# Decayed cumulative sum of a matmul: a new written order for the last 30 slots, and the last two output blocks copied in two pieces each

## The chip, the cores and the metric

The kernel runs on one core of a Trainium2 chip. The metric is the device time of one execution in microseconds (us). PE is the matrix engine, DVE the vector engine, ACT the scalar engine, POOL the GpSimd engine, and SP the engine whose queue issues the output stores here.

## The reference

```python
# x: (16, 2048, 1024), w: (1024, 1024), decay: (1024,), all float32
xw = x @ w
out[:, 0, :] = xw[:, 0, :]
for t in range(1, S):
    out[:, t, :] = decay[None, :] * out[:, t - 1, :] + xw[:, t, :]
```

A matrix product, and along the time axis of each batch a first-order recurrence with one decay per output column.

## The kernel before

**Tiling.** The time axis of each of the 16 batches is cut into 4 chunks of 512 rows: 64 chunks, numbered 0 to 63. Two neighbouring chunks make a group of 1024 rows, and each group is worked through in 8 **slots**, one for every 128 output columns. The last group is not worked in pairs: chunk 62 and chunk 63 get 8 slots each, of 512 rows ("half slots"). That makes 31 x 8 + 16 = 264 slots. In the agenda the last ones are numbered from the end: slots -32 to -17 are full, slots -16 to -1 are half.

**Input.** `load` (line 105, issued from POOL's queue) brings a quarter of a chunk as bf16 into `xb`. `turn` (line 115, DVE, letter T with the chunk's number) transposes it in 32 x 32 blocks into `xw`, and `part` (line 123, ACT, letters X and Y for the two halves) copies it into `xt`, the form that the matmul takes. `L` issues the next load, if one is left.

**Matmul.** `matmul` (line 131) makes 16 instructions of 128 x 512 for a full slot, 8 for a half slot, into PSUM. Full slots take turns on three `ps` buffers. Half slots take turns on the same three, except each fourth one (slots -13, -9, -5), which takes `spare`. PE may thus begin a full slot only when the slot three before it has left its buffer; slot -14 takes the buffer of slot -17.

**After the matmul**, a slot goes one of two ways.

- *Solo*: DVE scans all elements straight from PSUM (`run`, line 221, letter S).
- *Paired*: the recurrence is taken over every second element with the square of the decay. ACT copies the PSUM tile to `xs` (`copy`, line 183, letter p) and makes decay times its even-numbered elements into `h` (`odd`, line 169, letter g); then the PSUM buffer is free. POOL adds `h` to the odd elements (`join`, line 196, letter j), DVE scans half as many elements (line 201, letter S), ACT multiplies the result by the decay (`even`, line 169, letter h), and POOL adds the even elements (`fill`, line 246, letter c). `zero` (letter z) first sets the start element of the tile: with a POOL memset (line 190) at the start of a batch, otherwise with an ACT copy (line 192).

In both ways ACT saves the last column for the next chunk (`save`, line 250, letter k), where there is one. `back` (line 258, DVE, letter B) transposes the finished tile `so` back into an output tile `ot`; when the four slots of an outlet are back, four stores (line 279) go out on SP's queue. The tiles have rings: `so` 4, `xs` 3, `h` 4, `ot` 4 buffers.

Every fourth slot is solo by rule; `flips` turns a slot's way around.

```python
            self.paired = n % R != R - 1
            if len(tiles) in flips or len(tiles) - len(slots) in flips:
                self.paired = not self.paired
```

**Order.** Each engine runs its instructions in the order in which the program records them. While slot s is being multiplied, the deeds of its entry in `agenda` are recorded, as a string: "S-25 c-27" means the scan of slot -25, then the fill of slot -27. Slots without an entry follow `usual`, the steady pattern: copy, odd, zero and join of slot s, the scan of the slot before, and so on, then the turns and parts that are due (`later`).

**Ending.** The last four half slots (-4 to -1) are not transposed by DVE. `ending` (letter V) transposes them on PE into four blocks of 128 rows x 512 columns in PSUM (`cross`, line 383), and `leave` copies each block to SBUF (line 387; ACT for blocks 0 and 2, DVE for 1 and 3) and stores it (line 389). Slot -1 is multiplied and scanned in two halves (letters a and b).

Of the kernel before, what the change touches and what calls it, by code (L numbers as in the profile page):

```python
# [14 lines left out]
def _ap(ap_obj: bass.AP, new_ap, extra_offset=0):  # L15
    return dataclasses.replace(
        ap_obj,
        ap=[list(p) for p in new_ap],
        offset=ap_obj.offset + extra_offset,
    )  # L20
# [5 lines left out]
def kernel(  # L26
# [26 lines left out]
    nc = tc.nc  # L53
    pin = tc.keep_in_program_order
    B, S, D = x.shape
    assert w.shape == (D, D)

    NQ = 4
# [7 lines left out]
    R = K // 2  # L66
# [9 lines left out]
    def ring(pool, name, count, shape, dtype=FP32):  # L76
        i = turns[name] = turns.get(name, -1) + 1
        return pool.tile(shape, dtype, name=f"{name}{i % count}")
# [62 lines left out]
    class Tile:  # L141
# [39 lines left out]
        def copy(self):  # L181
            self.xs = sb.tile([128, 2 * TL], FP32, name=f"xs{self.lot % 3}")[:, 0:self.T]
            pin(nc.scalar.copy(out=self.xs, in_=self.ps))  # L183
# [141 lines left out]
    for q in range(NQ):  # L325
        pin(nc.sync.dma_start(
            out=rows[q * P:q * P + R],
            in_=_ap(decay, [[P, R], [CH, 2], [1, P]], q * CR)))
# [42 lines left out]
    def ending(i):  # L371
        b, t0 = chunks[-1]
        nb = TL // 128
        pts = [ring(psp, name, count, [128, R, 128])
               for name, count in (("spare1", 1), ("ps", 3), ("ps", 3), ("spare", 1))]
        wides = [ring(sb, *spot, [128, NQ, R, P])
                 for spot in (("xb", 3), ("xb", 3), ("xb", 3), ("h", 4))]

        def cross(blocks, rs):
            for i in blocks:  # L380
                for r in rs:
                    t = 2 + i * 128
                    pin(nc.tensor.transpose(  # L383
                        out=pts[i][:, r], in_=tiles[r - R].so[:, t:t + 128], identity=ident))

        def leave(i, copy):
            pin(copy(out=wides[i].rearrange("p q r i -> p r q i"),
                     in_=pts[i].rearrange("p r (q i) -> p r q i", q=NQ)))
            pin(nc.sync.dma_start(
                out=_ap(out, [[D, 128], [1, CH]], (b * S + t0 + i * 128) * D + CH),  # L390
                in_=wides[i].rearrange("p q r i -> p (q r i)")))

        cross((0,), range(R))
        cross((1,), range(R))
        cross((2, 3), range(R - 1))
        cross((2, 3), (R - 1,))
        for i in range(nb):
            leave(i, (nc.scalar.copy, nc.vector.tensor_copy)[i % 2])

    slots = [(g, n) for g in groups[:-1] for n in range(K)]  # L400
    slots += [([c], n) for c in groups[-1] for n in range(K)]
    tiles = []

    def turn_and_load(c):
# [4 lines left out]
    loads = [(c, q) for c in (2, 3, 4) for q in range(NQ)]  # L409
# [33 lines left out]
    agenda = {  # L443
        -99: "M0 M1 U0 M2 M3 U1 U2 w0 W1 w2 W3 K0 K1 K2 K3 E0 E1 G0 E2 G1 E3 F2 G3 E4 E5 G4 E6 G5 E7 F6 G7 W4 w5 W6 W7 D E8 E9 G8 E10 G9 E11 F10 G11 E12 L E13 G12 L E14 G13 E15 L F14 G15",
        0: "p0 z0 W8 W9 W10 W11",
        1: "g0",
        2: "L S1 L",
        3: "p2 z2 L g2 j0 S3 w12 w13 L w14 L w15 k1",
        4: "j2 B1 d k3",
        5: "p4 L S0 L g4 S2 L k0 h0 j4 B3 h2",  # L450
        6: "k2 c0 T2 c2 p5 g5 B0 L X2 L",
# [24 lines left out]
        31: "h28 p30 c28 B26 g30 h29 B28 j30 z30",  # L476
        32: "c29 S31 S30 h30 B29 c30 p32 g32 z32 j32 B30 B31 L L",
        33: "p33 g33 z33 j33 S32 h32 c32 k32 L L",
        -20: "z-20",
        -19: "p-20 g-20",  # L480
        -18: "j-20 S-19 S-20 k-19 B-19",
        -17: "h-20 k-20 c-20 S-18 B-20 k-18",
        -16: "I S-17",
        -15: "z-15 B-18 k-17",
        -14: "p-15 g-15 B-17 z-14 j-15",
        -13: "p-14 S-16 g-14 j-14 S-15 k-16",
        -12: "S-13 h-15 k-15 c-15 S-14 k-13",
        -11: "p-12 B-13 h-14 B-15 g-12 c-14 k-14 B-16",
        -10: "j-12 B-14 z-12 S-12 z-10 S-11",
        -9: "p-10 k-12 g-10 h-12 B-11 j-10 k-11",  # L490
        -8: "S-9 c-12 S-10 k-9",
        -7: "z-7 B-12 h-10 k-10 B-9 c-10 S-8",
        -6: "p-7 g-7 B-10 j-7 B-8",
        -5: "S-7 S-6 h-7 c-7",
        -4: "z-4 S-5 B-7",
        -3: "p-4 B-6 g-4 B-5 j-4",
        -2: "S-3 S-4",
        -1: "S-2 h-4 c-4 a-1 b-1 V",
    }
    flips = (1, 13, 15, -19, -18, -16, -11, -8, -6, -3, -2)  # L500
    later = {}
    begun = {"T": 12, "X": 11, "Y": 11}
    for c in range(5, nch):
# [6 lines left out]
    def usual(s):  # L510
        paired = [t.paired for t in tiles]
        do = [f"P{s}"] if paired[s] else []
        if paired[s - 1]:
            do.append(f"S{s - 1}")
        if not paired[s]:
            do.append(f"S{s}")
        do.append(f"C{s - 1}")
        if paired[s - 2]:
            do.append(f"B{s - 2}")
        if not paired[s - 1]:  # L520
            do.append(f"B{s - 1}")
        return do + later.get(s, []) + ["L"] * (2 if len(loads) > NQ else 1)

    def rest(s):
        do = [f"S{s - 1}"] if tiles[s - 1].paired else []
        do.append(f"C{s - 1}")
        if tiles[s - 2].paired:
            do.append(f"B{s - 2}")
        return do + [f"B{s - 1}"] + later.get(s, []) + ["L"] * len(loads)

    def perform(do):
        for deed in do:
# [4 lines left out]
    for step, (g, n) in enumerate(slots):  # L537
        T = TL * len(g)
        left = step - len(slots)
        if n % R == 0:  # L540
            ns, nj = range(n, n + R), T // P
            outlets = [Outlet(ns, nj)]
        if left == -R:
            outlets = []
        if step == 0:
            heads = [ring(psp, "ps", 3, [128, T]) for _ in range(3)]
            firsts = [ps[:, 0:TL] for ps in heads] + [spares[0]]
            seconds = [ps[:, TL:T] for ps in heads] + [spares[1]]
            for j0, j1 in halves:
                for k in range(0, K, 2):  # L550
                    for i in range(R):
                        matmul(firsts[i], i, k, xt_of[0], j0 * P, j1 * P, pairs=xw_of[0])
            for k in range(1, K, 2):
                for i in range(R):
                    matmul(firsts[i], i, k, xt_of[0])
            for k0 in range(0, K, 2):
                for i in range(R):
                    for k in (k0, k0 + 1):
                        matmul(seconds[i], i, k, xt_of[1], 0, H * P,
                               pairs=xw_of[1] if k0 < 4 else None)  # L560
            for i in range(R):
                for k in range(K):
                    matmul(seconds[i], i, k, xt_of[1], H * P, TL, H * P,
                           pairs=xw_of[1] if i < 2 else None)
        if step < R:
            ps = heads[n] if n < 3 else tuple(spares)
        else:
            if step == K + 1:
                ps = nexts
            elif len(g) == 2 or n % R < 3:  # L570
                ps = ring(psp, "ps", 3, [128, T])
            else:
                ps = ring(psp, "spare", 1, [128, TL])
            todo = [(k, l) for k in range(K) for l in range(len(g))]
            if step < K:
                todo.sort(key=lambda kl: kl[0] % 2)
            elif step == K:
                todo = []
                nexts = ring(psp, "ps", 3, [128, T])
                for l in range(len(g)):  # L580
                    for i, both in enumerate((ps, nexts)):
                        for k in range(K):
                            matmul(both[:, l * TL:(l + 1) * TL], n + i, k, xt_of.get(g[l]),
                                   pairs=xw_of[g[l]] if g[l] in (3,) else None)
            elif step == K + 1:
                todo = []
            if left == -1:
                ps = tuple(both[:, t:t + TL // 2] for t, both in zip(
                    (0, TL // 2), (ps, ring(psp, "ps", 3, [128, TL]))))
                for t, half in zip((0, TL // 2), ps):  # L590
                    for k in range(K):
                        matmul(half, n, k, xt_of[g[0]], t, t + TL // 2, t)
                todo = []
            for k, l in todo:
                matmul(ps[:, l * TL:(l + 1) * TL], n, k, xt_of[g[l]])
        tiles.append(Tile(g, n, ps, outlets))
        do = agenda.get(step, agenda.get(left) if left >= -20 else None)
        if do is None:
            do = usual(step)
        else:  # L600
            do = do.split()
            if left == -20:
                do = rest(step) + do
        perform(do)
    assert not loads
# [28 lines left out]
```

## Time and profile before

| what | value |
|---|---|
| median of the runs | 905.73 us (4 runs, 905.30 to 905.99) |
| the profiled execution | 906.53 us, of which the span from first to last instruction is 904.8 us |
| PE busy | 896.4 us, 4201 matmuls |
| DVE, ACT, POOL busy | 825.7, 684.4 and 655.2 us |
| granted PE clock | 0.999 |
| bytes read, written | 138.42 and 134.22 MB |

The profile describes one execution. Times in it run from the first instruction of the span. An engine's busy time is the sum of its instructions; what a wait is worth shows only in the chain of waits and in the idle time of the engine that sets the end. In the timeline a row gives start and duration in us, then engine, line, operation and tiles; in square brackets stands the idle time ahead of it and who ended it.

### The profile page before, as it was taken

The page shows a single profiled execution, that of the slowest core. Times are in us where ns is not written, and L with a number is a line of the kernel's source. Part 1 is how long each engine was busy: PE and PEld are TensorE (multiplying, and loading weights), DVE is VectorE, ACT ScalarE, POOL GpSimd, SP SyncE. Part 2 cuts the span into 40 slices and gives each one's busy share as a digit, 9 for nine tenths or more (in the row PEclk, how much of TensorE's full clock was granted, in tenths as well). Part 3 has the DMA queues.
Part 4 walks back from the last instruction along what each step waited for, and adds up shares of the span by engine and source line. Part 5 has one row for each costly group of instructions (what it writes and reads, how often), then busy time and mean ns, then how long its engine had stood idle before and what let it go on. Part 6 is the DMA issues. An engine that isn't in the chain of part 4 may idle for free.

```text
span 904.8 us, 12070 instructions
## 1 busy us (share of the span) xinstructions
PE 896.4 (99%) x4201; PEld 410.9 (45%) x4201; DVE 825.7 (91%) x628; ACT 684.4 (76%) x951; POOL 655.2 (72%) x753
## 2 busy tenths in 40 slices
PE   8999999999999999999999999999999999999997
PEld 4544444444444444444444444444444444444444
DVE  4999998999999999999998999999999999999997
ACT  4889957877877877878778778778777787787742
POOL 7978678777767778777677677777777776776622
PEclk9999999999999999999999999999999999999999
DMA  9999999999999999999999999999999999999868
GB/s 186 194 214 216 230 241 213 215 237 235 254 248 256 246 254 251 245 237 231 221 237 227 222 231 230 231 227 227 231 228 226 234 232 222 230 227 211 176 143 233
DMA packets 402542, 204.77 MB, mean 226 GB/s; under 512 B 8752, under 2 KB 401456, under 8 KB 402480
## 3 DMA queue, kind: packets, MB, share of 16 engines
q1 hardware_dynamic: 265168, 134.76, 61.0%
q0 software_dynamic: 137024, 68.70, 56.6%
q8 instruction: 33, 0.54, 0.2%
q10 hardware_dynamic: 288, 0.52, 0.2%
q14 instruction: 29, 0.24, 0.1%
HBM read 138.42 MB, written 134.22 MB: 301 GB/s over the span
## 4 chain that ended last, share of the span: by engine, by line
PE 95%; DMA 1%; DVE 1%; issue 1%; ACT 1%; POOL 0%; DVEq 0%; POOLq 0%
PE ps L131 94%; PE spare L131 1%; DVE so L221 1%; DMA xb<-in_x_dram 1%; DMA ot<-in_w_dram 1%; ACT xs L183 0%; ACT xt L123 0%; DVE so L201 0%; POOL xs L196 0%; ACT h L169 0%; DVE ot L258 0%; PE spare L383 0%; POOL ot L295 0%; PE ps L383 0%; POOL xb L105 0%
## 5 line engine op out<-in xcount | busy, mean ns | idle before, releaser
L131 PE MATMUL ps<-xt,wsb 128*128 128x512 bf16 x4024 | 867.8, 378 | 1.0 <-DVE wsb L302 0.9
L131 PEld LDWEIGHTS <-wsb 128*128 128x128 bf16 x4152 | 405.9, 98 | 480.6 <-DVE wsb L302 1.1
L196 POOL TENSOR_TENSOR xs<-h,xs 128x512 f32<-128x512 f32 (+1 forms) x189 | 241.8, 1280 | 190.4 <-ACT h L169 84.9
L183 ACT COPY xs<-ps 128x1024 f32<-128x1024 f32 (+1 forms) x189 | 188.7, 998 | 154.7 <-PE ps L131 150.2
L258 DVE STREAM_TRANSPOSE ot<-so 128x1024 f32<-128x1024 f32 (+1 forms) x260 | 300.1, 1191 | 2.1 <-POOL so L190 1.1
L246 POOL TENSOR_TENSOR so<-h,xs 128x512 f32<-128x512 f32 (+1 forms) x189 | 240.5, 1274 | 44.3 <-ACT h L169 28.1
L123 ACT COPY xt<-xw 128x2048 bf16<-128x2048 bf16 (+1 forms) x136 | 242.2, 1789 | 7.8 <-DVE xw L115 7.8
L105 POOL DMA_DIRECT2D xb<-in_x_dram x264 | 174.0, 660 | 3.2 <-DMA ot<-in_w_dram 1.1
L169 ACT ACTIVATE h<-so,dec 128x512 f32<-128x512 f32 (+1 forms) x189 | 144.9, 767 | 27.9 <-DVE so L201 24.7
L115 DVE STREAM_TRANSPOSE xw<-xb 128x2048 f32<-128x2048 f32 (+1 forms) x78 | 147.3, 1901 | 7.1 <-DMA xb<-in_x_dram 7.1
L201 DVE TENSOR_TENSOR_SCAN so<-spare,keep,xs 128x512 f32<-128x512 f32 (+1 forms) x96 | 119.3, 1244 | 26.9 <-POOL xs L196 26.6
L201 DVE TENSOR_TENSOR_SCAN so<-spare,xs 128x512 f32<-128x512 f32 x93 | 113.2, 1219 | 27.4 <-POOL xs L196 24.6
L169 ACT ACTIVATE h<-ps,dec 128x512 f32<-128x512 f32 (+1 forms) x189 | 129.6, 686 | 0.0
L221 DVE TENSOR_TENSOR_SCAN so<-dec,ps 128x1024 f32<-128x1024 f32 x34 | 76.8, 2260 | 1.0 <-ACT h L169 1.0
L221 DVE TENSOR_TENSOR_SCAN so<-dec,keep,ps 128x1024 f32<-128x1024 f32 (+1 forms) x36 | 77.2, 2145 | 0.4 <-PE ps L131 0.2
L250 ACT COPY keep<-so 128x1 f32<-128x1 f32 x136 | 25.3, 189 | 13.0 <-DVE so L221 12.6
L192 ACT COPY so<-keep 128x1 f32<-128x1 f32 x96 | 18.2, 191 | 2.0 <-DVE ot L258 1.8
L131 PE MATMUL ps<-xw,wsb 128*128 128x256 bf16 (+1 forms) x68 | 11.2, 301 | 0.1
L190 POOL MEMSET so<- 128x1 f32 x93 | 10.6, 116 | 0.4 <-DVE ot L258 0.4
L131 PE MATMUL spare<-xt,wsb 128*128 128x512 bf16 (+1 forms) x48 | 10.0, 335 | 0.0
L295 POOL DMA_DIRECT2D ot<-in_w_dram x12 | 6.5, 545 | 3.9 <-DMA xb<-in_x_dram 3.0
L320 PE MATMUL spare<-idle 128*128 128x512 bf16 x22 | 6.5, 465 | 1.2 <-DVE idle L310 1.2
(37 smaller groups left out, 36.4 us busy)
## 6 DMA issues: line engine op xcount, KB each, us to landing
out_dram<-ot SPq DMA_DIRECT2D x248, 512.0 KB, 10.9
xb<-in_x_dram POOLq DMA_DIRECT2D x248, 256.0 KB, 7.8
out_dram<-ot SPq DMA_DIRECT2D x12, 256.0 KB, 4.1
xb<-in_x_dram POOLq DMA_DIRECT2D x16, 128.0 KB, 6.3
ot<-in_w_dram POOLq DMA_DIRECT2D x12, 128.0 KB, 5.1
out_dram<-xb SPq DMA_DIRECT2D x3, 256.0 KB
ot<-in_w_dram ACTq DMA_DIRECT2D x2, 256.0 KB, 5.4
ot<-in_w_dram SPq DMA_DIRECT2D x2, 256.0 KB, 5.0
```

The source lines that it names most:

```text
L105: pin(nc.gpsimd.dma_start(out=xb_of[c][quad(q), j0:j1], in_=_ap(x, [[D, P], [P * D, j1 - j0], [1, CQ]], (b * S + t0 + j0 * P) * D + q * CQ)))
L115: pin(nc.vector.transpose(out=dst.rearrange("p (m j i) -> p j m i", m=M, i=P)[:, j0:j1, m0:m1], in_=src.rearrange("p (j m c) -> p j m c", ...
L123: pin(copy(out=xt_of[c][:, m0:m1, :, j0 * P:j1 * P], in_=src))
L131: pin(nc.tensor.matmul(out=ps[:, t0:t1] if ps.shape[1] >= t1 else ps, lhsT=lhs, rhs=rhs, start=(k == 0 and t0 == start), stop=(k == K - 1),))
L169: pin(nc.scalar.activation(out=h, in_=src, func=mybir.ActivationFunctionType.Copy, scale=dec[:, self.n:self.n + 1]))
L183: pin(nc.scalar.copy(out=self.xs, in_=self.ps))
L196: pin(nc.gpsimd.tensor_tensor(out=odds, in0=self.g, in1=odds, op=ALU.add))
L201: pin(nc.vector.tensor_tensor_scan(out=so[:, 3:T + 2:2], data0=squares[-1][:, n:n + 1].to_broadcast([128, T // 2]), data1=self.xs[:, 1:T:2 ...
L221: pin(nc.vector.tensor_tensor_scan(out=so[:, t + 2:t + 2 + size], data0=dec[:, n:n + 1].to_broadcast([128, size]), data1=ps, initial=befor ...
L246: pin(nc.gpsimd.tensor_tensor(out=self.so[:, 2:T + 2:2], in0=self.h, in1=self.xs[:, 0:T:2], op=ALU.add))
L250: pin(nc.scalar.copy(out=self.keep, in_=self.so[:, self.T + 1:self.T + 2]))
L258: pin(nc.vector.transpose(out=outlet.ot[:, :, c0:c0 + P], in_=self.so[:, 2 + t0:2 + t0 + nj * P].rearrange("p (i t) -> p i t", t=P)))
```

## The change

Three things change.

1. The agenda's entries for slots -20 to -1 are replaced by entries for slots -30 to -1. `rest`, which closed the steady pattern at slot -20, is gone; the steady pattern now ends with slot -31.
2. `flips` for the last slots shrinks. Solo before: -29, -25, -21, -19, -18, -17, -16, -13, -11, -9, -8, -6, -5, -3, -2, -1. Solo after: -29, -25, -21, -17, -13, -9, -7, -5, -3, -2, -1.
3. `leave` copies blocks 2 and 3 in two instructions each: the columns of slots -4, -3, -2 first, then those of slot -1. The store of a block is still one.

```diff
-        def leave(i, copy):
-            pin(copy(out=wides[i].rearrange("p q r i -> p r q i"),
-                     in_=pts[i].rearrange("p r (q i) -> p r q i", q=NQ)))
+        def leave(i, copy, pieces):
+            for r0, r1 in pieces:
+                pin(copy(out=wides[i].rearrange("p q r i -> p r q i")[:, r0:r1],
+                         in_=pts[i][:, r0:r1].rearrange("p r (q i) -> p r q i", q=NQ)))
...
-            leave(i, (nc.scalar.copy, nc.vector.tensor_copy)[i % 2])
+            leave(i, (nc.scalar.copy, nc.vector.tensor_copy)[i % 2],
+                  ((0, R),) if i < 2 else ((0, R - 1), (R - 1, R)))
...
-        -20: "z-20",
-        -19: "p-20 g-20",
-        -18: "j-20 S-19 S-20 k-19 B-19",
-        -17: "h-20 k-20 c-20 S-18 B-20 k-18",
-        -16: "I S-17",
-        -15: "z-15 B-18 k-17",
-        -14: "p-15 g-15 B-17 z-14 j-15",
...
-        -5: "S-7 S-6 h-7 c-7",
-        -4: "z-4 S-5 B-7",
-        -3: "p-4 B-6 g-4 B-5 j-4",
+        -30: "z-30 X61 Y61 L",
+        -29: "B-32 p-30 g-30 S-31 j-30 h-31 L",
+        -28: "z-28 S-30 c-31 S-29 h-30 c-30 B-31 L",
+        -27: "p-28 B-30 g-28 z-27 j-28 B-29 S-28 L",
+        -26: "z-26 p-27 T62 h-28 g-27 c-28 j-27 B-28 X62 L",
+        -25: "S-27 p-26 g-26 h-27 j-26 L",
+        -24: "z-24 S-25 Y62 c-27 S-26",
+        -23: "B-27 h-26 p-24 c-26 B-25 g-24 z-23 T63 j-24",
+        -22: "p-23 B-26 g-23 X63 j-23 S-24 z-22 S-23",
+        -21: "h-24 p-22 c-24 g-22 B-24 h-23 j-22 k-23 Y63",
+        -20: "c-23 S-21 k-24 z-20 S-22 k-21",
+        -19: "B-23 h-22 k-22 p-20 c-22 B-21 g-20 z-19 B-22 j-20 I",
+        -18: "p-19 z-18 S-20 g-19 h-20 j-19 k-20 c-20 S-19",
+        -17: "p-18 B-20 g-18 h-19 j-18 k-19 c-19 S-18",
+        -16: "z-16 S-17 k-18 h-18",
+        -15: "c-18 p-16 g-16 B-19 j-16 k-17",
+        -14: "p-15 g-15 S-16 z-15 j-15 B-18 h-16",
+        -13: "k-16 p-14 c-16 B-17 g-14 z-14 j-14",
+        -12: "B-16 S-14 z-12 S-15 k-14 h-14",
...
+        -7: "p-8 B-12 g-8 B-11 k-10 h-10 j-8 B-9 z-8",
+        -6: "c-10 S-8 B-10 h-8 S-7 c-8 z-6",
+        -5: "p-6 g-6 B-8 j-6 B-7",
+        -4: "z-4 S-6 S-5 h-6",
+        -3: "c-6 p-4 g-4 B-5 j-4 B-6",
         -2: "S-3 S-4",
         -1: "S-2 h-4 c-4 a-1 b-1 V",
     }
-    flips = (1, 13, 15, -19, -18, -16, -11, -8, -6, -3, -2)
+    flips = (1, 13, 15, -7, -3, -2)
...
-        do = agenda.get(step, agenda.get(left) if left >= -20 else None)
+        do = agenda.get(step, agenda.get(left) if left >= -30 else None)
...
-            if left == -20:
-                do = rest(step) + do
```

## The prediction

> **What bounds the kernel now.** I read the page's busy times first, then the chain of waits, then what PE waited for, then the timeline of the last 85 us.
>
> ```profile
> PE 896.4 (99%) x4201; PEld 410.9 (45%) x4201; DVE 825.7 (91%) x628; ACT 684.4 (76%) x951; POOL 655.2 (72%) x753
> ...
> PE 95%; DMA 1%; DVE 1%; issue 1%; ACT 1%; POOL 0%; DVEq 0%; POOLq 0%
> ```
> PE is on the chain for 95% of the span. That it is *busy* 99% would not be enough, so the next view asks for its idle time: engine, line, whom it waited for, then us in total, times, longest.
>
> ```profile
> PE spare L320 <- DVE idle L310: 1.2, 1, 1.2
> PE spare L320 <- ACT gate L336: 1.1, 1, 1.1
> PE ps L131 <- DVE wsb L302: 0.9, 1, 0.9
> PE ps L131 <- DVE so L221: 0.2, 1, 0.2
> ```
> The first three are in the start-up (lines 302 to 336). Only the fourth lies in the 30 slots that are replanned. So **no order of these slots can give back more than 0.2 us on PE**. The timeline (start, us, engine, line, operation) shows where it is, and the end:
>
> ```profile
> 871.15 2.25 DVE L221 TENSOR_TENSOR_SCAN so<-dec,ps 128x1024 f32<-128x1024 f32 x1
> ...
> 873.45 1.89 PE L131 MATMUL ps<-xt,wsb 128*128 128x512 bf16 x8 [0.17 <-DVE so L221]
> ...
> 894.42 1.28 DVE L221 TENSOR_TENSOR_SCAN so<-dec,keep,ps 128x512 f32<-128x512 f32 x1
> 895.62 0.73 DVE L201 TENSOR_TENSOR_SCAN so<-spare,keep,xs 128x256 f32<-128x256 f32 x1
> ...
> 896.26 1.26 DVE L221 TENSOR_TENSOR_SCAN so<-dec,keep,ps 128x512 f32<-128x512 f32 x1
> ...
> 898.26 0.75 DVE L221 TENSOR_TENSOR_SCAN so<-dec,so,ps 128x256 f32<-128x256 f32 x1
> ...
> 899.78 0.59 ACT L387 COPY xb<-ps 128x512 f32<-128x512 f32 x1 [0.62 <-PE ps L383]
> 899.89 0.69 DVE L387 COPY h<-spare 128x512 f32<-128x512 f32 x1 [0.18 <-PE spare L383]
> 900.90 0.39 SPq L389 DMA_DIRECT2D out_dram<-h  x1
> ```
> 24 matmuls take 5.18 us (876.90 to 882.08), so 0.2159 us each: a full slot is 16 of them, 3.454 us, a half slot 1.727 us. Counted back from the gap, PE ends slot -17 at 869.83, slot -20 at 859.47, slot -30 at 824.93. The gap of 0.17 us is slot -14 waiting for the bank that slot -17's scan (871.15) still read. At the end S-3, S-4, S-2 and the two half scans of slot -1 follow each other without a pause, then transposes, copies, four stores; the last, issued at 900.90, lands at 903.21 by the trace.
>
> [...]
>
> **Part 1, the pairing.** A paired slot costs DVE 1.22 us (L201) instead of 2.25 (L221), and adds copy 1.01, odd 0.69 and even 0.77 on ACT and two POOL adds of 1.29. At half size: DVE 0.72 for 1.25; ACT 0.58 + 0.48 + 0.53 + 0.19; POOL 2 x 0.74. Slots -19, -18 (full), -16, -11, -8, -6 (half) become paired, -7 becomes solo: two full and three half net. DVE loses 2 x 1.03 + 3 x 0.53 = 3.7 us; ACT gains 2 x 2.47 + 3 x 1.78 = 10.3; POOL 2 x 2.68 (a memset of 0.1 each included) + 3 x 1.48 = 9.8. The cover for it, by stretches (us, then PE, PEld, DVE, ACT, POOL busy):
>
> ```profile
> 860.00:870.00 10.00, 10.00 (x48) 4.56 (x47) 9.01 (x7) 3.57 (x6) 3.01 (x4) 1.00 0.68 136
> 870.00:880.00 10.00, 9.83 (x47) 4.38 (x45) 10.00 (x11) 4.60 (x15) 2.23 (x4) 1.00 0.62 141
> 880.00:890.00 10.00, 10.00 (x48) 4.53 (x47) 9.97 (x14) 4.13 (x15) 4.32 (x6) 1.00 0.96 241
> ```
> ACT and POOL have more than half of this stage free, so the added work is hidden as throughput: nothing. The 3.7 us that DVE saves are off the path too, except where DVE holds a bank. What counts is **latency**: a paired bank is free after copy and odd, but the finished tile passes through ACT, POOL, DVE, ACT, POOL, DVE, each in its written order.
>
> **Part 2, the orders.** The queues are the same up to DVE's turn of chunk 61 (ends 824.63), so I went through them from there with the trace's start-to-start times: ACT copy 0.91, odd 0.58, even 0.68, part 1.81; DVE paired scan 1.20 or, first in its batch, 1.14, solo 2.2, back 1.16, turn 2.22; POOL add 1.25; 0.04 to 0.09 us from an end to the engine it releases. Three places are tight.
>
> *Slots -30 and -29.* Both parts of chunk 61 stand ahead of p-30 on ACT: 824.68 + 2 x 1.81 = 828.30 for a copy that PE had ready at 824.93. Queued behind: g-30 to 829.90, POOL's join to 831.27, and DVE, which has B-32 and S-31 done by 828.35 and stands idle until S-30 at 831.31. S-29 (solo) then ends at 834.83; PE wants its bank at 835.29. Margin 0.4 us. p-30's own bank is free at 829.9, wanted at 831.83.
>
> *Slot -26.* ACT puts X62 (after T62, 841.69) ahead of p-26: 843.55, odd ends 845.15; PE wants the bank at 845.65. Margin 0.45 us.
>
> *Slot -17.* S-21 ends 860.36, S-22 861.5; h-22 stands ahead of p-20, so p-20 starts 862.36, g-20 ends 863.96, the join 865.33, S-20 866.59, h-20 867.45; then p-18, g-18 to 869.04, its join to 870.41, S-18 to 871.67, S-17 871.58 to 873.84. Slot -14 starts at 873.89 instead of 873.28: a gap of **0.6 us against 0.17 now, +0.4**. What DVE saved by pairing -19 and -18 it spends waiting for joins.
>
> Later nothing binds. DVE reaches S-3 some 0.05 us after PE has slot -3 ready, as now, since B-5 and B-6 end about then (their fill needs S-6, at 892.4). So the end moves with PE.
>
> *SP's queue.* The group -20..-17 is complete at 877.95 instead of 875.68. Its four stores hold SP until about 883.8, so the next group (now from 881.68) goes out 2 us late, and the one after about 1.4 us late. The trace has a pause there: SP finished a group at 892.6 and the next began at 894.35. It takes up most of it; I carry 0 to 0.7 us, and take 0, because the half group's last store landed at 899.49, ahead of the last blocks' data. POOL's queue holds no loads any more there: all issue earlier, as before.
>
> **Part 3, the copies in two pieces.** Since both pieces wait for the same last transpose, nothing starts earlier. [...] ACT's ends gate the third store, so +0.05 on the end; DVE's has 0.3 us to spare, since SP's own 0.4 us comes in between. Bounds: -0.3 (if the first piece could run early) to +0.15; I take +0.05.
>
> **Sum.** +0.44 + 0.05 = about +0.5 us on the profiled execution (906.53 us, span 904.8); that one ran 0.8 above the median of 905.73, so the forecast is 905.73 + 0.5 = **906.2 us**. A measurement can tell about 0.2%, 1.8 us, from no change.
>
> **Rivals.**
> *The gap closes (0.28).* If my hops are 0.05 us too long each, S-17 ends in time: -0.17 + 0.05, so 905.6; with the copies early, 905.3. For it: joins and scans in the steady stage follow within 0.04 us. Against: DVE idles in that walk three times.
> *Slower (0.15).* One mechanism: DVE comes late to slot -29. PE waits as soon as the chain X61, Y61, p-30, join, S-30, S-29 is 0.4 us longer than walked, and since DVE catches up nothing between -24 and -17 (it waits for joins), S-17's gap grows beside it. With 0.1 to 0.2 us more on each of its ten hops, 0.6 to 1.6 us at -26 and the 0.6 us at -14: over 1.8 us once the chain is some 1.7 us longer; 907.6 to 909. The stores' 0.7 us would come on top. Against: each duration is measured, and DVE, ACT and POOL repeat theirs within 0.05 us.
> *The change does not do what it says:* the split buys no overlap, as argued; that is in the forecast.
> *Faster by over 0.2% (0.02)* would need 1.8 us where PE has 0.17 to give and the end a few tenths.
>
> The likeliest case, with 0.55, spans 905.9 to 907.0; with the bounds of the stores and copies and a part of the slower case the range is **905.2 to 907.7**. Chances: faster 0.02, within 0.2% 0.83, slower 0.15.
>
> **What would show it.** PE's waits: one line for L221 of 0.4 to 0.8 us before slot -14, none for ACT. DVE idle near 829 and ACT's p-30 some 3 us after PE. L201 counts up by five, L221 down; two copies per last block with the same start as now. I am wrong if PE waits in several slots, if the span past PE's last matmul of L131 grows by over 1 us, or if the time falls by over 1 us.

## The result, and the profile after

| | before | after |
|---|---|---|
| median of the runs | 905.82 us (58 runs, 905.10 to 907.24) | 907.15 us (40 runs, 906.52 to 908.03) |
| profiled execution, its span | 906.53, 904.8 us | 907.46, 905.7 us |

The ratio is 1.0015, with a 95% interval of 1.0010 to 1.0019: **1.3 us slower**. That is below the 1.8 us that the prediction called no change, and the interval leaves out zero. The forecast was 906.2 us (905.2 to 907.7).

First the page of the kernel after: busy times, and the two rows of the paired scan (line 201).

```profile
PE 897.4 (99%) x4201; PEld 411.2 (45%) x4201; DVE 822.3 (91%) x629; ACT 693.2 (77%) x970; POOL 664.8 (73%) x765
...
L201 DVE TENSOR_TENSOR_SCAN so<-spare,keep,xs 128x512 f32<-128x512 f32 (+1 forms) x99 | 121.2, 1227 | 27.7 <-POOL xs L196 27.2
L201 DVE TENSOR_TENSOR_SCAN so<-spare,xs 128x512 f32<-128x512 f32 x95 | 115.5, 1218 | 27.8 <-POOL xs L196 25.0
```
194 paired scans instead of 189 (96 and 93 in these two rows before), so five slots more; DVE is 3.4 us less busy (3.7 forecast), ACT 8.8 more (10.3), POOL 9.6 more (9.8).

Next what PE waited for in the kernel after (engine, line, whom; us in total, times, longest), and the timeline of the replanned slots.

```profile
PE ps L131 <- DVE so L221: 0.3, 1, 0.3
```

```profile
828.12 1.00 ACT L183 COPY xs<-ps 128x1024 f32<-128x1024 f32 x1
...
831.18 1.28 DVE L201 TENSOR_TENSOR_SCAN so<-spare,keep,xs 128x512 f32<-128x512 f32 x1 [3.02 <-POOL xs L196]
832.38 2.32 DVE L221 TENSOR_TENSOR_SCAN so<-dec,keep,ps 128x1024 f32<-128x1024 f32 x1
...
871.15 2.26 DVE L221 TENSOR_TENSOR_SCAN so<-dec,ps 128x1024 f32<-128x1024 f32 x1
873.46 1.89 PE L131 MATMUL ps<-xt,wsb 128*128 128x512 bf16 x8 [0.33 <-DVE so L221]
...
894.51 1.24 DVE L221 TENSOR_TENSOR_SCAN so<-dec,keep,ps 128x512 f32<-128x512 f32 x1
...
898.30 0.75 DVE L221 TENSOR_TENSOR_SCAN so<-dec,so,ps 128x256 f32<-128x256 f32 x1
899.23 2.08 SPq L390 DMA_DIRECT2D out_dram<-xb  x3
899.82 0.65 ACT L388 COPY xb<-ps 128x384 f32<-128x384 f32 x2 [0.61 <-PE ps L383]
899.93 0.76 DVE L388 COPY h<-spare 128x384 f32<-128x384 f32 x2 [0.18 <-PE spare L383]
901.41 0.60 SPq L390 DMA_DIRECT2D out_dram<-h  x1
```
The walk through slot -30 was right to 0.2 us: p-30 at 828.12 (828.30 forecast), S-30 after 3.0 us of idle DVE, S-29 done at 834.70, PE not held at -26 or -23. The gap before slot -14 is 0.33 us instead of 0.17. From one and the same matmul, 3500 before the last one of line 131, to the end of that last one, PE needs 754.36 us, before 754.20. **PE accounts for 0.16 us.**

The rest comes after it. From the end of PE's last matmul of line 131 ("PE's end") to the end of the span it is 7.87 us, before 6.95: **0.92 us**. The last scan, transposes and copies stand where they stood. What differs is SP's row: its three `xb` stores take 2.08 us together, against this row of the timeline of before:

```profile
899.19 1.62 SPq L389 DMA_DIRECT2D out_dram<-xb  x3
```
Before, each of the four stores of the last blocks took 0.35 to 0.39 us to issue; here the first takes 0.76. The page's list of DMA issues has the same in small: the median time from issue to landing (last column) of the 256-KB stores rose from 4.1 us.

```profile
out_dram<-ot SPq DMA_DIRECT2D x12, 256.0 KB, 4.7
```
The next view is what the DMA engines did, by stretches (us; busy time of PE, PEld, DVE, ACT, POOL with instructions; PE's clock, DMA share, GB/s). First before, then after.

```profile
876.00:884.00 8.00, 8.00 (x38) 3.63 (x37) 7.97 (x11) 4.71 (x16) 3.45 (x5) 1.00 0.83 187
884.00:892.00 8.00, 8.00 (x38) 3.62 (x37) 8.00 (x11) 2.46 (x8) 3.10 (x5) 1.00 0.99 255
892.00:900.00 8.00, 7.85 (x51) 4.95 (x49) 7.60 (x11) 2.29 (x5) 1.47 (x2) 1.00 0.93 214
900.00:904.00 4.00, 0.00 (x0) 0.00 (x0) 0.58 (x1) 0.36 (x1) 0.00 (x0) 0.77 0.73 269
```

```profile
876.00:884.00 8.00, 8.00 (x38) 3.63 (x37) 7.65 (x11) 5.74 (x21) 4.68 (x7) 1.00 0.62 136
884.00:892.00 8.00, 8.00 (x38) 3.62 (x37) 7.98 (x12) 3.95 (x12) 4.58 (x7) 1.00 0.98 253
892.00:900.00 8.00, 7.89 (x51) 4.93 (x49) 7.67 (x11) 2.79 (x6) 2.21 (x3) 1.00 1.00 238
900.00:904.00 4.00, 0.00 (x0) 0.00 (x0) 0.68 (x2) 0.47 (x2) 0.00 (x0) 0.99 0.97 321
```
In the first stretch the kernel after moves (187 - 136) x 8 us = 0.41 MB less; in the second the engines are full in both; in the third it has no slack left (1.00 against 0.93) and makes up (238 - 214) x 8 = 0.19 MB; some 0.2 MB are still to go at 900, at the rates shown 0.6 to 0.9 us of work (an estimate). Summed over the trace's DMA packets, 1.59 MB are still to come at PE's end before, 1.80 after. The deferred bytes are those of the group of slots -20 to -17 (four stores of 512 KB). SP issues the first of them at 875.68 before, at 877.47 after. From there to the last landing 6.3 MB go out (4 x 512 + 16 x 256 KB), in 28.2 us before (903.83) and 27.3 after (904.77). The timeline of SP's queue from 893.5 on, before and then after (a row takes in the stores that follow one another closely):

```profile
894.35 3.20 SPq L279 DMA_DIRECT2D out_dram<-ot  x4
```

```profile
893.09 5.67 SPq L279 DMA_DIRECT2D out_dram<-ot  x5
```
The groups of four slots are named by their first slot. Before, SP finished group -12 at 892.6, paused 1.75 us, and group -8 went out from 894.35. After, SP is still issuing group -12 at 894.05, the pause is down to 0.56 us, and group -8's last store lands at 902.34 instead of 901.07, 3.1 us after SP issued the first block's store (899.23) instead of 1.9.

### The profile page after: what moved, and what is told of

The parts are those of the page before. It is cut to its first block, busy times and chain, and to the rows that moved or that the text cites. A ratio compares the mean times of both kernels' runs of the same rounds, so it can differ in the third digit from the quotient of the medians.

```text
span 905.7 us, 12111 instructions
## 1 busy us (share of the span) xinstructions
PE 897.4 (99%) x4201; PEld 411.2 (45%) x4201; DVE 822.3 (91%) x629; ACT 693.2 (77%) x970; POOL 664.8 (73%) x765
## 5 line engine op out<-in xcount | busy, mean ns | idle before, releaser
L131 PE MATMUL ps<-xt,wsb 128*128 128x512 bf16 x4024 | 868.0, 378 | 1.1 <-DVE wsb L302 0.6
L131 PEld LDWEIGHTS <-wsb 128*128 128x128 bf16 x4152 | 405.9, 98 | 480.8 <-issue 1.3
L196 POOL TENSOR_TENSOR xs<-h,xs 128x512 f32<-128x512 f32 (+1 forms) x194 | 246.9, 1273 | 174.2 <-ACT h L169 72.6
L183 ACT COPY xs<-ps 128x1024 f32<-128x1024 f32 (+1 forms) x194 | 192.4, 992 | 143.0 <-PE ps L131 138.4
L246 POOL TENSOR_TENSOR so<-h,xs 128x512 f32<-128x512 f32 (+1 forms) x194 | 245.5, 1267 | 50.0 <-ACT h L169 35.5
L169 ACT ACTIVATE h<-so,dec 128x512 f32<-128x512 f32 (+1 forms) x194 | 148.0, 764 | 33.5 <-DVE so L201 30.5
L201 DVE TENSOR_TENSOR_SCAN so<-spare,keep,xs 128x512 f32<-128x512 f32 (+1 forms) x99 | 121.2, 1227 | 27.7 <-POOL xs L196 27.2
L201 DVE TENSOR_TENSOR_SCAN so<-spare,xs 128x512 f32<-128x512 f32 x95 | 115.5, 1218 | 27.8 <-POOL xs L196 25.0
L169 ACT ACTIVATE h<-ps,dec 128x512 f32<-128x512 f32 (+1 forms) x194 | 132.6, 683 | 0.0
L221 DVE TENSOR_TENSOR_SCAN so<-dec,keep,ps 128x1024 f32<-128x1024 f32 (+1 forms) x33 | 73.4, 2225 | 0.1
L221 DVE TENSOR_TENSOR_SCAN so<-dec,ps 128x1024 f32<-128x1024 f32 x32 | 72.3, 2259 | 0.0
L131 PE MATMUL ps<-xw,wsb 128*128 128x256 bf16 (+1 forms) x68 | 11.2, 301 | 0.1
L131 PE MATMUL spare<-xt,wsb 128*128 128x512 bf16 (+1 forms) x48 | 10.0, 335 | 0.0
```

The costliest lines, as they stand in the source:

```text
L131: pin(nc.tensor.matmul(out=ps[:, t0:t1] if ps.shape[1] >= t1 else ps, lhsT=lhs, rhs=rhs, start=(k == 0 and t0 == start), stop=(k == K - 1),))
L169: pin(nc.scalar.activation(out=h, in_=src, func=mybir.ActivationFunctionType.Copy, scale=dec[:, self.n:self.n + 1]))
L196: pin(nc.gpsimd.tensor_tensor(out=odds, in0=self.g, in1=odds, op=ALU.add))
L201: pin(nc.vector.tensor_tensor_scan(out=so[:, 3:T + 2:2], data0=squares[-1][:, n:n + 1].to_broadcast([128, T // 2]), data1=self.xs[:, 1:T:2 ...
L221: pin(nc.vector.tensor_tensor_scan(out=so[:, t + 2:t + 2 + size], data0=dec[:, n:n + 1].to_broadcast([128, size]), data1=ps, initial=befor ...
L246: pin(nc.gpsimd.tensor_tensor(out=self.so[:, 2:T + 2:2], in0=self.h, in1=self.xs[:, 0:T:2], op=ALU.add))
```

## The experiments

**Theories.** *A*: the group of slots -20 to -17 is complete 1.8 us later; behind it the stores run with hardly a pause to the end, so the last blocks land later. *B*: the copies in two pieces cost it. *C*: PE's waits cost it. *D*: as A, but SP's issuing is the limit and not the DMA engines.

The table gathers what the traces show, relative to PE's end, and the medians. Each kernel ran beside the kernel before; the ratio is to those runs. In one profile the stretch after PE's end is good to some tenths of a us only (in e1 it is 0.37 longer than in before, the median 0.1), so the medians decide.

| kernel | median (before's beside it) | ratio [95%] | group -20 first issued | group -8 last landed | first last-block store | end of span |
|---|---|---|---|---|---|---|
| before | 905.82 | | -22.12 | 3.27 | 1.39 | 6.95 |
| after | 907.15 (905.82) | 1.0015 [1.0010, 1.0019] | -20.35 | 4.52 | 1.41 | 7.87 |
| e1_split_only | 905.95 (905.85) | 1.0001 [0.9992, 1.0009] | -22.12 | 3.98 | 1.38 | 7.32 |
| e2_plan_only | 907.39 (905.85) | 1.0016 [1.0009, 1.0022] | -20.35 | 4.68 | 1.41 | 8.04 |
| e3_before_late_back | 907.05 (905.85) | 1.0012 [1.0006, 1.0019] | -20.31 | 5.17 | 2.02 | 9.08 |
| e4_after_early_back | 907.73 (905.85) | 1.0021 [1.0014, 1.0028] | -21.34 | 5.39 | 2.67 | 8.76 |
| e5_before_no_store | 906.31 (905.82) | 1.0005 [0.9997, 1.0014] | -22.12 | 3.28 | 1.38 | 7.33 |
| e6_after_no_store | 906.77 (905.82) | 1.0010 [1.0002, 1.0019] | -20.35 | 4.10 | 1.40 | 7.74 |
| e9_before_back_between | 906.29 (906.18) | 1.0002 [0.9993, 1.0010] | -20.95 | 4.45 | 1.38 | 7.82 |
| e10_after_pool_stores | 907.82 (906.18) | 1.0019 [1.0012, 1.0025] | -20.35 | 4.85 (SP's two) | 1.41 | 8.50 |
| e11_before_pool_stores | 907.80 (906.18) | 1.0019 [1.0011, 1.0028] | -22.12 | 4.53 (POOL's two) | 1.38 | 8.70 |

**e1_split_only and e2_plan_only: the two halves of the change.** e1 is the kernel before with the two-piece copies; e2 is the kernel after with the single ones.

```diff
 # e1, on the kernel before; leave itself as in the change
 ...
-            leave(i, (nc.scalar.copy, nc.vector.tensor_copy)[i % 2])
+            leave(i, (nc.scalar.copy, nc.vector.tensor_copy)[i % 2],
+                  ((0, R),) if i < 2 else ((0, R - 1), (R - 1, R)))
 # e2, on the kernel after: these two lines the other way round
```

> The kernel before with blocks 2 and 3 copied in two pieces, the old orders kept. Theory A (late stores: the new order completes the output group of slots -20 to -17 some 1.8 us later, the pause in the output queue is gone and the last stores land 0.9 us later): no more than +0.1 us, since no output group moves. Theory B (the extra copies hold up the last stores): most of the loss is here, +0.5 to +0.9 us. Theory C (PE's wait for the bank of slot -17): 0. In the profile the two copies start when the single one did (A, B, C alike) and end 0.1 us later.

> The changed kernel with each of the last four blocks copied in one instruction again: the new orders and pairing alone. Theory A: +0.8 to +1.2 us over the kernel before, nearly all of the loss stays. Theory B: +0.2 us or less. Theory C: +0.2 us, PE's wait being 0.33 us against 0.17.

e1 is 0.1 us from the kernel before, e2 keeps 1.5 us (0.8 to 1.2 forecast under A): **B falls, the loss is in the plan.** The plan is the orders and the pairing together; no run parts the two. The pieces start where the single copies did (899.82 and 899.93 after, 899.78 and 899.89 before) and take 0.65 and 0.76 us instead of 0.59 and 0.69: they buy no overlap, and cost 0.06 and 0.07.

**e3_before_late_back: one transpose moved.** The kernel before, with the back of slot -17 two scans later; nothing else differs.

```diff
-        -14: "p-15 g-15 B-17 z-14 j-15",
-        -13: "p-14 S-16 g-14 j-14 S-15 k-16",
+        -14: "p-15 g-15 z-14 j-15",
+        -13: "p-14 S-16 g-14 j-14 S-15 B-17 k-16",
```

> The kernel before with one deed moved: the back of slot -17 stands behind the scans of slots -16 and -15, so that the output group of slots -20 to -17 is complete some 1.9 us later (about 877.5 instead of 875.7), as in the changed kernel. PE's work, pairing and all else are as before. Theory A: +0.6 to +1.0 us, the pause at 892.6 to 894.35 in the output queue disappears and the last store lands about 0.9 us later. Theories B and C: 0, within 0.2 us.

The group goes out at -20.31, within 0.04 us of the kernel after. PE's stretch is 754.20 us, as before; the last scans are not late. Yet the kernel is 1.2 us slower by the medians (0.6 to 1.0 forecast). Its profiled execution was 0.7 us over its median, so the 9.08 in the table is long for it. The timeline of its SP queue:

```profile
892.47 6.37 SPq L279 DMA_DIRECT2D out_dram<-ot  x5
...
898.94 2.12 SPq L389 DMA_DIRECT2D out_dram<-xb  x3
```
SP issues group -8 right up to 898.84, past the first block's copy (done at 898.29), and so begins the last blocks 0.6 us late; of the pause before group -8, 0.15 us are left. The DMA part of the page, in 40 slices of the window 870 to 902 (tenths busy), for before, after and e3 in turn:

```profile
DMA  9996200068889889999979999999998799998799
```

```profile
DMA  9999996100488898899999899999999999999999
```

```profile
DMA  9962000005888988999998999999999999897999
```
Before, the engines idle for three slices of 0.8 us (the zeros), and there are 7s and 8s among the 9s later on. After, the hole lies 2 us further right, and from 880 to the end, behind one 4, the digits are 8s and 9s without a 7. In e3 the hole is five slices wide (the group before it is stored as early as ever, this one late), and but for one 7 the digits behind it are 8s and 9s from 881 on. **One late transpose, ahead of which two scans move up by its 1.2 us and nothing else changes, gives 1.2 us by the medians, of the 1.3 to be explained.** That is A. The bytes still to come at PE's end, summed over each trace's packets, go with it: 1.59 MB in before and e1, 1.80 in after, 1.81 in e2, 1.83 in e3. At the 238 GB/s of the third stretch above, the 0.2 MB are 0.9 us (an estimate).

**e4_after_early_back: the reverse, on the kernel after.** B-17 brought forward again, with S-18 later and c-18 behind it.

```diff
-        -17: "p-18 B-20 g-18 h-19 j-18 k-19 c-19 S-18",
-        -16: "z-16 S-17 k-18 h-18",
-        -15: "c-18 p-16 g-16 B-19 j-16 k-17",
-        -14: "p-15 g-15 S-16 z-15 j-15 B-18 h-16",
-        -13: "k-16 p-14 c-16 B-17 g-14 z-14 j-14",
+        -17: "p-18 B-20 g-18 h-19 j-18 k-19 c-19",
+        -16: "z-16 S-17 S-18 k-17",
+        -15: "p-16 g-16 k-18 h-18 B-19 B-17 j-16 c-18",
+        -14: "p-15 g-15 B-18 S-16 z-15 j-15 h-16",
+        -13: "k-16 p-14 c-16 g-14 z-14 j-14",
```

> The changed kernel with the solo scan of slot -17 ahead of the scan of slot -18, and the backs of -19, -17, -18 ahead of the scan of slot -16. PE's wait before slot -14 should go (0.33 us to 0), and the output group -20 to -17 be complete at about 876.7 instead of 877.5. Theory A: -0.3 to -0.6 us against the changed kernel, in step with the 0.7 us by which the group is earlier. Theory C: -0.3 us from PE alone, with PE's end earlier by that much. Theory B: 0 apart from PE's 0.3.

A miss: the time rose. The gap before slot -14 did go, and the group came 1.0 us earlier (0.7 to 0.8 expected), but what DVE did earlier pushed its later scans back. What PE waited for in e4, from 800 us on:

```profile
PE spare L383 <- POOL so L246: 1.3, 1, 1.3
PE spare L131 <- DVE so L221: 0.6, 1, 0.6
```
PE waits 0.6 us at slot -9 for the scan of slot -13, and the last scan ends so late that the first block is stored at 2.67 us instead of 1.41. The lateness was moved, not removed: 1.9 us over before. It says nothing on A, because it delays the end by itself.

**e5_before_no_store and e6_after_no_store: less to store.** The group of slots -16 to -13 is not stored, in the kernel before (e5) and after (e6).

```diff
 # in store; ns_muted holds the outlet that is made at slot -16
+            if ns_muted and self is ns_muted[0]:
+                return
```

> The kernel before without the four stores (1 MB) of the output group of slots -16 to -13; all else as before, so the output lacks that part. It is the partner of the next run. Theory A: the output queue has some 4 us of air before the last groups; the time falls by 0 to 0.5 us against the kernel before. Theories B and C: no change.

> The changed kernel without the four stores of the group of slots -16 to -13 (that part of the output is left out). Theory A: the backlog that the late group -20 to -17 makes is gone before the last blocks, so the distance to the kernel before with the same stores left out shrinks from 1.3 us to 0.2 to 0.4 us (PE's 0.16 and the copies' 0.1). Theories B and C: the distance stays at 1.3 us.

With 1 MB less in the queue the two kernels lie 0.5 us apart instead of 1.3 (A forecast 0.2 to 0.4). Weak support by the times: the intervals of the two ratios overlap, and their difference, 0.0005, is no better known than to about 0.0012. The traces say more: at PE's end e6 has 1.66 MB still to come and e5 1.60, so 0.06 MB apart, where after and before are 0.21 apart. e5 did not gain on before: its median lies 0.5 us above, with an interval from -0.3 to +1.3 us. So no cost of before's own backlog shows.

**e7_before_two_queues and e8_after_two_queues: the last block's store on ACT's queue.**

```diff
-            pin(nc.sync.dma_start(
+            pin((nc.scalar if i == 3 else nc.sync).dma_start(
```

> The kernel before with the store of the last block issued from ACT's queue instead of SP's. It goes out when its copy ends, about 0.3 us sooner (2.8 instead of 3.1 us after PE's last matmul). Theory A with the DMA engines as the limit at the end: -0.1 to 0. Theory D (SP's issuing is the limit, not the engines): -0.3 us.

> The changed kernel with the store of the last block issued from ACT's queue. In the changed kernel SP issues it 0.7 us after its copy has ended, since SP was held by the late group of slots -8 to -5. Theory A (DMA engines): -0.1 to -0.3 us, the queued bytes being the same. Theory D (SP's issuing): -0.6 to -0.8 us.

Inconclusive on D: 917.2 and 917.3 us, ratio 1.0125 both [1.011, 1.014]. What SP waited for in e7:

```profile
SPq L279 <- DMA out_dram<-h: 13.3, 1, 13.3
```
In the trace the store on ACT's queue has the same DMA semaphore as the second store of group -12 on SP's queue, and SP issues that one only at 901.99, when ACT's store has landed (901.97); so SP stood 13.3 us, in e8 11.9. An edit of one engine's name created a wait across queues.

**e9_before_back_between: how much lateness is free.** As e3, with B-17 between the two scans.

```diff
-        -14: "p-15 g-15 B-17 z-14 j-15",
-        -13: "p-14 S-16 g-14 j-14 S-15 k-16",
+        -14: "p-15 g-15 z-14 j-15",
+        -13: "p-14 S-16 B-17 g-14 j-14 S-15 k-16",
```

> The kernel before with the back of slot -17 between the scans of slots -16 and -15: the group -20 to -17 is complete 1.2 us later, instead of 1.9 us in the run with the back behind both. Theory A: the pause of 1.75 us in the output queue takes up a part of it, so +0.2 to +0.7 us over the kernel before, less than the 1.2 us that the later back cost. Theories B and C: 0.

The group is 1.2 us late, and the medians move by 0.1 us (0.2 to 0.7 forecast): the pause of 1.75 us would take that up, and a limit between 1.2 and 1.8 us of lateness would follow. But the interval reaches from -0.6 to +0.9 us, and the one profile looks much like that of after: 0.64 us of the pause are left (after: 0.56), and the end is as long (7.82 to 7.87). The bytes still to come at PE's end, 1.71 MB, lie halfway between before and after, which speaks for a cost that grows with the lateness more than for a limit. Which it is stays open.

**e10_after_pool_stores and e11_before_pool_stores: two of group -8's stores on POOL's queue.** This takes two issues from SP just ahead of the last blocks and leaves the bytes.

```diff
-            outlets = [Outlet(ns, nj)]
+            outlets = [Outlet(ns, nj, queues=(nc.sync, nc.gpsimd) if left == -8 else (nc.sync,))]
 # e11 also, on the kernel before
-        -3: "p-4 B-6 g-4 B-5 j-4",
+        -3: "p-4 B-6 g-4 j-4 B-5",
```

> The changed kernel with two of the four stores of the group of slots -8 to -5 issued from POOL's queue instead of SP's, so that SP is free for the last blocks. The bytes and the moment at which they are ready are the same. Theory A with the DMA engines as the limit: the last blocks' stores go out earlier, yet land no more than 0.2 us earlier. Theory D (SP's issuing is the limit): the last stores leave 0.5 us earlier and the time falls by 0.4 to 0.6 us.

> The kernel before with two of the four stores of the group of slots -8 to -5 issued from POOL's queue (the join of slot -4 recorded ahead of the back of slot -5, so that it isn't held up). SP is not behind here, so theory A gives no change (within 0.2 us), theory D -0.3 us at most. If it comes out ahead, it is the version that beats both.

SP's queue in e10:

```profile
891.83 4.50 SPq L279 DMA_DIRECT2D out_dram<-ot  x4
...
898.99 3.02 SPq L390 DMA_DIRECT2D out_dram<-xb  x3
```
SP has issued its last `ot` store at 896.33 and stands free for 2.66 us. Still its three `xb` stores take 3.02 us, the second alone 1.62, and the kernel is no faster than after (907.82; 1.6 us over before). **Nothing speaks for D.** The kernel after itself speaks against it: SP has issued group -8's last store by 898.76, ahead of the end of the first block's copy (899.21), and the DMA engines are busy for 1.00 and 0.97 of the last two stretches shown above, so the limit lies behind the issue. e11 was a miss: no change was expected, and moving two stores of the kernel *before* cost 1.6 us (1.0011 to 1.0028). So stores from POOL's queue have a price of their own here, and e10 by itself can't settle D: in e11 too, where SP was never behind, the three `xb` stores take 2.74 us. The trace of e11 shows part of the price: POOL issues its two stores at 893.98 and 894.64, the first packet on its queue starts at 897.80, and the stores land 5.8 and 7.1 us after issue, where the four of this group on SP's queue before took 3.2 to 4.8. Why they start so late stays open.

No kernel of these was faster than before.

## Why the prediction was right, and where it was not

- **What bounds the kernel: right.** Only 0.17 us were to be had on PE, and no version got below before.
- **Part 1, pairing at nothing: right as throughput.** The work appeared on ACT and POOL (8.8 and 9.6 us) and no wait of PE for them. Whether its latency is what made the group of slots -20 to -17 late, or the new order of the transposes, no run shows.
- **Part 2, the orders on PE: right in place, too large.** The gap was put before slot -14 with 0.6 us; it is 0.33. S-17 was walked to 871.58 and came at 871.15. Some 0.15 us of that are the execution as a whole, which ran that much earlier (PE was ready for slot -14 at 873.13, not 873.28). The rest came between slot -29 and slot -20: p-20 began at 861.98, not 862.36. From there to S-18 (870.01, walked to about 870.45) the hops were too long by 0.06 us in all, so the first rival's 0.05 us on each is not what these hops show. The term of +0.44 measured +0.16.
- **Part 2, SP's queue: the step that failed.** "I carry 0 to 0.7 us, and take 0, because the half group's last store landed at 899.49, ahead of the last blocks' data." The later group was foreseen (877.95; it came at 877.47) and so was the pause that it eats (1.2 of its 1.75 us). The reason for the zero was a misreading: 899.49 is the first of the 16 landings that the trace has for this store. The last came at 901.07, 1.9 us *after* the first block's store was issued (899.19). So already before, the last blocks were behind that group, with nothing to spare; in the same way the last store's "903.21" is 903.83 in full. The term measures 0.92 us in the profile less what the copies do in it, which is over the 0.7 that was its bound. e3 prices it by itself at 1.2 us of medians (0.5 to 1.7).
- **Part 3, the copies: +0.05 forecast, +0.06 and +0.07 each in the trace, +0.1 by e1's median with an interval that holds zero.** "Nothing starts earlier" held. In the trace of after the columns of slots -4 to -2 of block 2 had been transposed by 899.35, and ACT stood idle for 0.61 us, yet its first piece started at 899.82, behind the block's last transpose (899.51 to 899.78); on DVE it is the same (899.93, behind 899.62 to 899.89). What held the pieces, the trace doesn't tell. The forecast's +0.05 was the author's estimate; no run had shown it.
- **The sum.** +0.5 forecast, +0.93 in the profiled execution, +1.3 by the medians. The total is inside the range because the range took in the stores' bound; the likeliest case by itself (905.9 to 907.0) misses it by 0.15 us. Its sign was right for a reason that gave about an eighth of it (0.16 of 1.3), and so by luck; the rest was in the term taken as nothing.
- **The rivals.** DVE was not late to slot -29 (3.0 us of idle time ahead of S-30, and no wait of PE). Of the signs of being wrong, "the span past PE's last matmul of L131 grows by over 1 us" came within a tenth in the profile (0.92); by the medians, 1.3 less PE's 0.16, it is passed.

The 0.4 us between the one profile (+0.93) and the medians (+1.3) come from which executions were profiled: before's was 0.7 us over its median, after's 0.3. Open: where lateness of a group begins to cost; whether the pairing or the order made the group late; and why POOL's stores start late.

## What to carry to other kernels

When the engine that bounds the kernel is full to its end, look at what drains behind it. A tile that is off the path, and only finished 1.8 us later, cost 1.2 us here (e3), because what was stored behind it kept the DMA engines busy almost to the end (in e3 for 0.8 or more of every slice but one from 881 to 902); so in a reordering, walk the output queue to the last byte as carefully as the bounding engine. And read a store as landed only when all 16 of its landings are there: first and last lay 1.6 us apart in the very number that decided here.

## What the runs showed of the hardware

- Near the end, with the DMA engines busy for 0.98 or more of a stretch of 8 us, stores in 512-byte packets (`ot`) moved at 0.24 to 0.26 MB/us (before and after); the last blocks' 2-KB packets, once no `ot` packet was left, at 0.36 (901 to 903 us before, 361 GB/s) and 0.35 (902 to 904 after, 346).
- Of four stores of 256 KB that SP issued one after another, the first took 0.32 us to issue and the fourth 1.2: in before (group -8, after the pause of 1.75 us) 0.32, 0.52, 0.98 and 1.24, and in e5, where the DMA engines had stood idle ahead of them, 0.32, 0.49, 1.03 and 1.22. So here a long issue row came without a backlog of earlier groups.
- Two stores of 256 KB issued from POOL instead of SP took 1.31 us to issue, began to move 3.8 us after the first was issued, and the kernel before was 1.6 us slower with them (e11, where the join of slot -4 is also recorded ahead of the back of slot -5).
- A store moved from SP's to ACT's queue held SP for 13.3 us (e7) and 11.9 us (e8) through a DMA semaphore that both used.
